# Hybrid attention encoder layer: keys, query reloads, denominators and w_out's rows moved in fewer, larger transfers

## The chip, the cores and the metric

The kernel runs on one core of one Trainium2 chip. The metric is the device time of one execution in microseconds. Three runs of the kernel before took 2543.44, 2537.59 and 2541.20 us, median 2541.2.

## What is computed

One encoder layer over x of 2048 tokens by 1024 columns, all in float32. An RMS norm and one projection give two head groups with 8 query heads and 2 key/value heads each, 64 columns a head. Group A attends over all tokens, group B over a window of 128 tokens to either side with a learned sink per head. Both go through one output projection, and a SwiGLU feed-forward part of 2816 columns follows. Cut to what matters here:

```python
h = rms_norm(x, norm_mix_pre[l])
qa, ka, va, qb, kb, vb = jnp.split(h @ w_in[l], SPLITS, axis=-1)
out_a = global_attention(rope(rms_norm(qa)), rope(rms_norm(ka)), va)
out_b = window_attention(rope(qb), rope(kb), vb, sink_b[l])     # den = sum(e) + exp(sink - m)
mixed = jnp.concatenate([rms_norm(out_a, group_norm_a[l]),
                         rms_norm(out_b, group_norm_b[l])], axis=-1) @ w_out[l]
x = x + rms_norm(mixed, norm_mix_post[l])
f = (jax.nn.silu(h2 @ w_gate[l]) * (h2 @ w_up[l])) @ w_down[l]  # h2: the norm of the new x
x = x + rms_norm(f, norm_ffn_post[l])
```

## The kernel before

The tokens are cut into 16 tiles of 128. Every float32 product is made of three or so passes over a high and a low half of its operands (names that end in h and l, or hi and lo).

**Projections, to about 412 us.** `proj` runs tile t through w_in into three PSUM banks (pp); `evac` copies them to nat on ScalarE. `rope` rotates queries and keys on VectorE and GpSimd, `heads(t)` transposes them. From there the keys of group A go to the DRAM scratch KD, the queries of group A to QA (high halves and low halves of both groups side by side), and the queries of group B are moved within SBUF into RB, four transfers of 64 rows a tile. Two tiles behind, group B is attended: `bmax` makes each head's maximum, negates it (mr) and moves it with the sink's exponentials (eh) into rows of R2B below the copied queries; `battn` makes scores, exponentials and output (o); `den_row` copies each group's row of denominators to rb and moves it to cmp, 8 rows of 64 a group, `recip` inverts cmp and writes it to RDB, `spread` reads it back over 64 partitions a group into rb, and `bfin` multiplies (oT) and stores OB. In tiles 4 to 11 `w_out_prep(k)` also loads part k of w_out in two halves of columns (woraw), scales and splits it (wohi on ScalarE, wolo on VectorE) and stores it to WO.

**Sweep of group A, to about 1200 us.** `attn` goes over 16 query tiles x 2 groups x 16 key tiles. `load_q(t)` reads R1 (group A's queries, high and low halves stacked) and R2 (the halves the other way round) from QA, called when tile t-1 is half done. The denominators go the same way as in group B, by the names cmpa, RDA and dena; the multiplication is oa<-oa,dena. The output projection runs beside it.

**Feed-forward, to the end**, with its own loads; the change does not touch it.

All transfers are issued by SyncE's queue. The order of all instructions on every engine comes from a planner (`Plan`, L257): it lays the recorded operations out by a table of costs, in which a transfer costs its bytes over 350 bytes a ns and 1100 ns, and SyncE 590 ns an issue, whatever its shape; the instructions then run on each engine in that order. Since one helper records them all, nearly all rows have the line L527, and one goes by the names.

`load` is one DMA. `ROWS` are the lower and upper 64 partitions. What sets a transfer's shape is the slice or rearrangement given to it, as here in `spread` and `w_out_prep` before:

```python
for g in range(2):
    src = scratch[8 * g:8 * g + 8].rearrange("(o c) x -> o (c x)", o=1)
    self.load(rb[ROWS[g]], src.broadcast_to([HD, 512]))
...
for h in range(2):
    self.load(raw[ROWS[h]], self.i["w_out"][r0 + 256 * h:r0 + 256 * h + HD, n * 512:(n + 1) * 512])
```

Of the kernel before, what the change touches and what calls it, by code (L numbers as in the profile page):

```python
# [18 lines left out]
P = 128  # L19
# [4 lines left out]
HD = 64  # L24
# [26 lines left out]
EARLY = 4  # L51
EARLY_NS = 2000
KV_NS = 3500
ES_ROW = 96
B0 = 432
B_TAIL = 13
T0_BANKS = (("mm", "ow", "o1"), ("mm", "a1", "a2"))
# [28 lines left out]
def f32(ap):  # L86
    return ap.bitcast(F32)
# [442 lines left out]
class Layer:  # L530
# [281 lines left out]
    def b_consts(self):  # L812
        nc, bp = self.nc, self.bp
        self.G = self.wp.tile([P, 2, 2, HD], F32, tag="G", bufs=1, name="G")
        for j, nm in enumerate(("q_norm_a", "k_norm_a")):
            self.bcast_row(self.G[:, j, 0, :], self.i[nm])
            self.bcast_row(self.G[:, j, 1, 0:32], self.i[nm][32:64])
            self.bcast_row(self.G[:, j, 1, 32:64], self.i[nm][0:32])
        nc.vector.tensor_scalar(self.G[:, 0], self.G[:, 0], 0.125, self.down_s, op0=ALU.mult, op1=ALU.mult)
        self.band = bp.tile([P, 3 * P], F32, tag="band", bufs=1, name="band")  # L820
        nc.gpsimd.memset(self.band, 0.0)
        for cs, sg in ((slice(0, P), 1), (slice(2 * P, 3 * P), -1)):
            nc.gpsimd.affine_select(out=self.band[:, cs], in_=self.band[:, cs], pattern=[[sg, P]],
                                    compare_op=ALU.is_ge, fill=-3.0e38, base=0, channel_multiplier=-sg)
        self.NR = 5
        self.VB = [bp.tile([P, 2, 2, P], F32R, tag=f"VB{r}", bufs=1, name=f"VB{r}") for r in range(self.NR)]
        self.K2B = [bp.tile([HD + 1, 2, P], F32R, tag=f"K2B{r}", bufs=1, name=f"K2B{r}") for r in range(self.NR)]
        for r in range(self.NR):
            nc.gpsimd.memset(f32(self.VB[r])[:, :, 0, HD:], 1.0)
            nc.gpsimd.memset(f32(self.VB[r])[:, :, 1, HD:], 0.0)  # L830
            nc.gpsimd.memset(f32(self.K2B[r])[HD:HD + 1], 1.0)
        self.va = [self.wp.tile([P, 2, 192], F32R, tag=f"va{r}", bufs=1, name=f"va{r}") for r in range(1)]
        for r in range(1):
            nc.gpsimd.memset(f32(self.va[r])[:, :, P:], 1.0)
        self.K1B, self.RB = {}, {}
        self.R2 = bp.tile([ES_ROW + 2, 2, 512], F32R, tag="R2B", bufs=1, name="R2B")
        nc.gpsimd.memset(f32(self.R2)[HD:ES_ROW + 2], 0.0)
        self.zs = bp.tile([ES_ROW + 2, P], F32R, tag="zs", bufs=1, name="zs")
        nc.gpsimd.memset(f32(self.zs), 0.0)
        nc.gpsimd.memset(f32(self.zs)[ES_ROW:ES_ROW + 2, HD:P], 1.0)  # L840

# [24 lines left out]
    def w_in_tiles(self, j):  # L868

        if j < 4:  # L870
            return [self.wk.tile([P, 512], F32R, tag=f"ks{3 * j + n}", bufs=1, name="w_in") for n in range(3)]
        w = (self.wk if j < 8 else self.wq).tile([P, 1536], F32R, tag=f"kv{j}", bufs=1, name="w_in")
        return [w[:, n * 512:(n + 1) * 512] for n in range(3)]

    def urgent(self, ns):
        if self.plan:
# [131 lines left out]
    def heads(self, t):  # L1008

        nc, wp, bp = self.nc, self.wp, self.bp  # L1010
        ra, rb = self.roped
        RB = bp.tile([P, 2, 512], F32R, tag="RB", bufs=3, name="RB")
        tk = self.mm_bank()[:, 0:2 * P].rearrange("p (a c) -> p a c", a=2)
        for j, src in ((1, rb), (0, ra)):
            nc.tensor.transpose(out=tk[:, j, :], in_=src[:, 8:10, :].rearrange("p h d -> p (h d)"),
                                identity=self.ident)
        KA = wp.tile([P, 2, P], F32R, tag="K1A", bufs=1, name="KA")
        nc.scalar.activation(KA[:, 0, :], tk[:, 0, :], AF.Copy)
        nc.vector.tensor_tensor(KA[:, 1, :], tk[:, 0, :], f32(KA)[:, 0, :], op=ALU.subtract)
        kd = self.k_part(self.KD[t // 2], t % 2).rearrange("p (g c) -> p g c", g=2)  # L1020
        k2b = self.K2B[t % self.NR]
        dst = []
        for s in ((t - 4) // 4, t // 4, (t + 4) // 4):
            pos = t - (4 * s - 1)
            if 0 <= s < NT // 4 and 0 <= pos < 6:
                if s not in self.K1B:
                    self.K1B[s] = bp.tile([P, 2, 6 * P], F32R, tag="K1B", bufs=2, name="K1B")
                dst.append(self.K1B[s][:, :, pos * P:(pos + 1) * P])
        for g in range(2):
            for h in range(2):  # L1030
                for d in dst:
                    nc.scalar.activation(d[ROWS[h], g, :], tk[ROWS[g], 1, :], AF.Copy)
            for h in range(2):
                self.load(kd[ROWS[g if h == 0 else 1 - g], g, :], f32(KA)[ROWS[g], h, :])
            nc.vector.tensor_tensor(k2b[0:HD, g, :], tk[ROWS[g], 1, :], f32(dst[0])[ROWS[g], g, :], op=ALU.subtract)
        yield 218
        for src, R in ((rb, RB), (ra, None)):
            tp = self.mm_bank()
            for p in range(4):
                nc.tensor.transpose(out=tp[:, p * P:(p + 1) * P],  # L1040
                                    in_=src[:, 2 * p:2 * p + 2, :].rearrange("p h d -> p (h d)"), identity=self.ident)
            HL = wp.tile([P, 2, 512], F32R, tag="RA", bufs=1, name="HL")
            nc.scalar.activation(HL[:, 0, :], tp, AF.Copy)
            nc.vector.tensor_tensor(HL[:, 1, :], tp, f32(HL)[:, 0, :], op=ALU.subtract)
            if R is None:
                self.load(self.QA[t], f32(HL))
            else:
                for g in range(2):
                    for h in range(2):
                        self.load(f32(R)[ROWS[g if h == 0 else 1 - g], g, :], f32(HL)[ROWS[g], h, :])  # L1050
            yield 436
        self.RB[t] = RB

# [7 lines left out]
    def bmax(self, t):  # L1061
# [1 line left out]
        nc, bp, sm = self.nc, self.bp, self.sm  # L1063
        RB = self.RB[t]
        R2 = self.R2
        for g in range(2):
            self.load(f32(R2)[0:HD, g, :], f32(RB)[ROWS[g], g, :])
        lo = 1 if t == 0 else 0
        hi = 2 if t == NT - 1 else 3
        n = (hi - lo) * P  # L1070
# [119 lines left out]
    def shifts(self):  # L1190

        nc, sm = self.nc, self.sm
        for t in range(NT):
            RA = [self.kv.tile([P, 512], F32R, tag="pha", bufs=NPH, name="RAs") for g in range(2)]
            for g in range(2):
                for h in range(2):
                    self.load(f32(RA[g])[ROWS[g if h == 0 else 1 - g]], self.QA[t][ROWS[g], h, :])
            mx = sm.tile([P, 8, 4], F32, tag="mx4", name="mx4")
            for h in range(8):
                g, p = h // 4, h % 4  # L1200
# [18 lines left out]
    def load_q(self, t):  # L1219
        if t >= NT or t in self.qt:  # L1220
            return
        R1 = self.kv.tile([P, 2, 512], F32R, tag="R1", name="R1")
        for g in range(2):
            for h in range(2):
                self.load(f32(R1)[ROWS[g if h == 0 else 1 - g], g, :], self.QA[t][ROWS[g], h, :])
        self.qt[t] = R1
        for g in range(2):
            R2 = self.wk.tile([P, 512], F32R, tag=f"ks{8 + (2 * t + g) % 4}", bufs=1, name="R2")
            for h in range(2):
                self.load(f32(R2)[ROWS[1 - g if h == 0 else g]], self.QA[t][ROWS[g], h, :])  # L1230
            self.qs[t, g] = R2

    def load_shift(self, t):
        self.sh_row[t] = self.kv.tile([1, 2, 512], F32R, tag="shr", bufs=1, name="shr")
# [30 lines left out]

    def den_row(self, rb, src, cmp, g):

        row = rb[HD * g:HD * g + 1]
        self.nc.scalar.activation(row, src[HD:HD + 1], AF.Copy)
        self.load(cmp[8 * g:8 * g + 8], row.rearrange("o (c x) -> o c x", x=HD))  # L1270

    def recip(self, cmp, scratch):
        self.nc.vector.reciprocal(cmp, cmp)
        self.load(scratch, cmp)

    def spread(self, rb, scratch):
        for g in range(2):
            src = scratch[8 * g:8 * g + 8].rearrange("(o c) x -> o (c x)", o=1)
            self.load(rb[ROWS[g]], src.broadcast_to([HD, 512]))

    def normalize(self, o, den, j):
        cs = slice(j * P, (j + 1) * P)
# [114 lines left out]
    def w_out_prep(self, k):  # L1397

        nc, bp = self.nc, self.bp
        r0 = 512 * (k // 4) + HD * (k % 4)  # L1400
        for n in range(2):
            raw = bp.tile([P, 512], F32, tag="pf", bufs=2, name="woraw")
            for h in range(2):
                self.load(raw[ROWS[h]], self.i["w_out"][r0 + 256 * h:r0 + 256 * h + HD, n * 512:(n + 1) * 512])
            hi = bp.tile([P, 512], F32R, tag="ph", bufs=PB, name="wohi")
            lo = bp.tile([P, 512], F32R, tag="pl", bufs=PB, name="wolo")
            nc.scalar.activation(hi, raw, AF.Copy, scale=self.gg[:, k:k + 1])
            nc.vector.scalar_tensor_tensor(lo, raw, self.gg[:, k:k + 1], f32(hi), op0=ALU.mult, op1=ALU.subtract)
            self.load(self.WO[2 * n][:, k], f32(hi))
            self.load(self.WO[2 * n + 1][:, k], f32(lo))  # L1410
            yield 500
# [425 lines left out]
```

## Time and profile before

| | |
|---|---|
| median of 3 runs | 2541.2 us (2537.59 to 2543.44) |
| the profiled execution | 2536.24 us, of which the span from first to last instruction 2534.4 us |
| TensorE matmuls busy | 2451.9 us (97%) |
| VectorE, GpSimd, ScalarE busy | 1894.7 us (75%), 1471.7 us (58%), 1392.5 us (55%) |
| mean share of the 16 DMA engines | 42.9% by the main queue, 349.40 MB in 200704 packets |
| mean granted TensorE clock | 0.993 of full |

The profile is of one execution. PE is TensorE, PEld its weight loads, ACT ScalarE, DVE VectorE, POOL GpSimd, SP SyncE. An engine's idle time costs something only where the engine that bounds the time waits for it in the end; which engine that is, is read for each stretch by itself.

### The profile page before, as it was taken

How to read it: one execution, taken by the hardware profiler on the slowest of the kernel's cores; microseconds unless marked ns; L12 is line 12 of the kernel's file. 1: busy time of each engine (PE TensorE's matmuls, PEld its weight loads, DVE VectorE, ACT ScalarE, POOL GpSimd, SP SyncE). 2: the span in 40 equal slices, each digit the busy share in tenths (PEclk: the TensorE clock that was granted, in tenths of full speed). 3: DMA queues.
4: the chain of work that ended last, by engine and by line, in shares of the span. 5: the costliest groups of instructions: out<-in, count | busy, mean ns of one | idle time of the engine just before them, and what ended most of it. 6: DMA issues, size and time to landing. Idle time of an engine off the chain costs nothing. (4 is left out here: it accounts for less than half of the span.)

```text
span 2534.4 us, 34148 instructions
## 1 busy us (share of the span) xinstructions
PE 2451.9 (97%) x10604; PEld 1946.2 (77%) x10604; DVE 1894.7 (75%) x2864; ACT 1392.5 (55%) x2610; POOL 1471.7 (58%) x1175
## 2 busy tenths in 40 slices
PE   8999999899999999999899999999999999999997
PEld 6777777567777777777688888878888888888886
DVE  6777776888898989898876776796656656556655
ACT  5666665797888888787433333353233334433433
POOL 4444333488889998999365566746546444331433
PEclk9999999999999999999999999999999999999999
DMA  6555545252221313231544444563333228554664
GB/s 208 152 174 166 168 144 168 80 195 65 76 80 58 106 59 104 96 121 63 195 135 145 162 154 162 190 222 104 101 107 104 92 79 278 175 182 143 194 189 153
DMA packets 200895, 351.66 MB, mean 139 GB/s; under 512 B 26624, under 2 KB 82304, under 8 KB 200192
## 3 DMA queue, kind: packets, MB, share of 16 engines
q1 hardware_dynamic: 200704, 349.40, 42.9%
q8 instruction: 85, 1.39, 0.2%
q14 instruction: 106, 0.87, 0.1%
HBM read 229.85 MB, written 106.56 MB: 133 GB/s over the span
## 5 line engine op out<-in xcount | busy, mean ns | idle before, releaser
L527 POOL TENSOR_TENSOR acc<-acc,pha 128x512 f32<-128x512 f32 x408 | 561.0, 1389 | 36.5 <-ACT pha L527 15.6
L527 POOL TENSOR_TENSOR s<-wraw 128x512 f32<-128x512 f32 x88 | 122.5, 1407 | 304.2 <-DMA wraw<-in_w_up_dram 184.3
L527 PE MATMUL gu<-xh,wl 128*128 128x512 f32 x776 | 288.4, 397 | 4.5 <-DVE wl L527 4.5
L527 PE MATMUL gu<-xl,wh 128*128 128x512 f32 x776 | 291.5, 396 | 0.0
L527 PE MATMUL gu<-xh,wh 128*128 128x512 f32 x776 | 287.4, 396 | 0.0
L527 DVE TENSOR_TENSOR pla<-mm,pha 128x512 fp32r<-128x512 f32 x370 | 246.4, 682 | 39.6 <-ACT pha L527 30.1
L527 PE MATMUL mm<-R,kt 128*128 128x512 f32 x740 | 256.0, 403 | 8.8 <-DVE pla L527 7.7
L527 ACT ACTIVATE wh<-s 128x512 fp32r<-128x512 f32 x176 | 110.6, 630 | 278.4 <-PE gu L527 141.4
L527 PE MATMUL pp<-w_in,xh 128*128 128x512 f32 x720 | 237.1, 403 | 12.6 <-ACT w_in L527 9.4
L527 DVE TENSOR_TENSOR al<-ar,ah 128x512 fp32r<-128x512 f32 x154 | 134.3, 874 | 149.3 <-ACT ah L527 128.5
L527 POOL TENSOR_TENSOR c<-c,c 128x512 f32<-128x512 f32 x132 | 201.7, 1542 | 69.5 <-DVE c L527 40.2
L527 ACT ACTIVATE mm<-mm 128x512 f32<-128x512 f32 x370 | 214.9, 590 | 29.1 <-PE mm L527 25.6
L527 ACT ACTIVATE ah<-ar 128x512 fp32r<-128x512 f32 x154 | 97.1, 630 | 220.2 <-PE gu L527 144.8
L527 DVE TENSOR_TENSOR c<-gu,c 128x512 f32<-128x512 f32 x174 | 116.4, 686 | 115.5 <-PE gu L527 114.1
L527 DVE TENSOR_TENSOR wl<-s,wh 128x512 fp32r<-128x512 f32 x176 | 175.6, 1003 | 12.1 <-ACT wh L527 5.9
L527 ACT ACTIVATE wh<-wraw 128x512 fp32r<-128x512 f32 x132 | 83.1, 630 | 175.3 <-PE gu L527 95.2
L527 PEld LDWEIGHTS gu<-xh,wl 128*128 128x128 f32 x776 | 146.6, 189 | 39.6 <-DVE wl L527 5.4
L527 PEld LDWEIGHTS mm<-R,kt 128*128 128x128 f32 x740 | 134.7, 189 | 53.3 <-DVE pla L527 25.8
L527 PE MATMUL gv<-xl,wh 128*128 128x512 f32 x456 | 173.2, 394 | 0.3 <-DVE xl L527 0.3
L527 PEld LDWEIGHTS gu<-xl,wh 128*128 128x128 f32 x776 | 146.4, 189 | 34.5
L527 PE MATMUL ow<-wo,oh 128*128 128x512 f32 x488 | 171.0, 396 | 1.8 <-DVE mix L527 0.9
L527 PEld LDWEIGHTS gu<-xh,wh 128*128 128x128 f32 x776 | 146.3, 189 | 34.4 <-ACT wh L527 0.2
(257 smaller groups left out, 6494.1 us busy)
## 6 DMA issues: line engine op xcount, KB each, us to landing
AC<-c SPq DMA_DIRECT2D x154, 256.0 KB
ar<-AC SPq DMA_DIRECT2D x154, 256.0 KB
wdr<-in_w_down_dram SPq DMA_DIRECT2D x99, 256.0 KB
wraw<-in_w_gate_dram SPq DMA_DIRECT2D x20, 1024.0 KB
wraw<-in_w_up_dram SPq DMA_DIRECT2D x20, 1024.0 KB
R<-QA SPq DMA_DIRECT2D x128, 128.0 KB
st<-XB SPq DMA_DIRECT2D x40, 256.0 KB
xn<-in_x_dram SPq DMA_DIRECT2D x16, 512.0 KB
```

What stands on the lines that cost most here:

```text
L527: op.call(*[real(a) for a in op.args], **{k: real(v) for k, v in op.kw.items()})
```

## The change

Eight kinds of transfer are cut in another way. With the shapes of the issues before and after, a tile each (out shape; the count of 2 is that of the slowest dimension on either side):

- KD<-KA: 4 of 64x128 become 2 of 2x64x128 (both groups in one, the halves no longer swapped for group 1).
- RB<-HL: still 4 of 64x512, now to the same half for both groups. R2B<-RB: 2 of 64x512 become 1 of 64x1024.
- R<-QA: 8 of 64x512 become 4 of 64x2x512; the second queries of both groups share one buffer (kq0, kq1), which takes the place of two (ks8 to ks11).
- cmp<-rb and cmpa<-dena: 2 of 8x64 become 1, read as 2x8x64. rb<-RDB and dena<-RDA: 2 of 64x512 become 1 to 128 rows, read as 2x64x512 (the 64 without a step).
- woraw<-w_out: 4 of 64x512 become 2 to 128 rows, read as 2x64x512.
- R2B's rows for the sink move up from 96 to 65, so that the last matmul of the denominators contracts 67 rows instead of 98.

```diff
-ES_ROW = 96
+ES_ROW = HD + 1
...
+    def w_in_slot(self, i):
+        if i < 8:
+            return self.wk.tile([P, 512], F32R, tag=f"ks{i}", bufs=1, name="w_in")
+        if i % 2 == 0:
+            self.pair = self.wk.tile([P, 2, 512], F32R, tag=f"kq{(i - 8) // 2}", bufs=1, name="w_in")
+        return self.pair[:, i % 2, :]
...
+        for h in range(2):
+            self.load(kd[ROWS[h]].rearrange("r g c -> g r c"), f32(KA)[:, h, :])
         for g in range(2):
...
-            for h in range(2):
-                self.load(kd[ROWS[g if h == 0 else 1 - g], g, :], f32(KA)[ROWS[g], h, :])
...
-                        self.load(f32(R)[ROWS[g if h == 0 else 1 - g], g, :], f32(HL)[ROWS[g], h, :])
+                        self.load(f32(R)[ROWS[h], g, :], f32(HL)[ROWS[g], h, :])
...
-        for g in range(2):
-            self.load(f32(R2)[0:HD, g, :], f32(RB)[ROWS[g], g, :])
+        self.load(f32(R2)[0:HD], f32(RB)[0:HD])
...
-        for g in range(2):
+        R2 = self.wk.tile([P, 2, 512], F32R, tag=f"kq{t % 2}", bufs=1, name="R2")
+        parts = self.QA[t].rearrange("(g r) h c -> h r g c", g=2)
+        for R, a in ((R1, 0), (R2, 1)):
             for h in range(2):
-                self.load(f32(R1)[ROWS[g if h == 0 else 1 - g], g, :], self.QA[t][ROWS[g], h, :])
+                self.load(f32(R)[ROWS[h ^ a]], parts[h])
...
-        row = rb[HD * g:HD * g + 1]
-        self.nc.scalar.activation(row, src[HD:HD + 1], AF.Copy)
-        self.load(cmp[8 * g:8 * g + 8], row.rearrange("o (c x) -> o c x", x=HD))
+        self.nc.scalar.activation(rb[HD * g:HD * g + 1], src[HD:HD + 1], AF.Copy)
+        if g == 1:
+            rows = rb.rearrange("(g r) (c x) -> g r c x", g=2, x=HD)[:, 0]
+            self.load(cmp, rows)
...
-        for g in range(2):
-            src = scratch[8 * g:8 * g + 8].rearrange("(o c) x -> o (c x)", o=1)
-            self.load(rb[ROWS[g]], src.broadcast_to([HD, 512]))
+        src = scratch.rearrange("(g c) x -> g (c x)", g=2)
+        self.load(rb, src.unsqueeze(1).broadcast_to([2, HD, 512]))
...
-            for h in range(2):
-                self.load(raw[ROWS[h]], self.i["w_out"][r0 + 256 * h:r0 + 256 * h + HD, n * 512:(n + 1) * 512])
+            rows = self.i["w_out"].rearrange("(a r) c -> a r c", r=256)[2 * (k // 4):2 * (k // 4) + 2]
+            self.load(raw, rows[:, HD * (k % 4):HD * (k % 4) + HD, n * 512:(n + 1) * 512])
```

The planner lays the whole program out anew. Two places are shown, both in tile 8, where part 4 of w_out is prepared.

SyncE before, from the move of group B's queries to the transfer of the negated maxima (x4 is four issues in a row):

```order
L527 DMA RB<-HL 64x512 x4
L527 DMA woraw<-in_w_out_dram 64x512 x4
L527 DMA R2B<-RB 64x512
L527 DMA QA_64<-HL 128x1024
L527 DMA KD_76<-KA 64x128
L527 DMA WO_89<-wohi 128x512
L527 DMA cmp<-rb 8x1x64
L527 DMA WO_91<-wohi 128x512
L527 DMA WO_90<-wolo 128x512
L527 DMA WO_92<-wolo 128x512
L527 DMA R2B<-mr 1x8x128
```

SyncE with the change, the same place:

```order
L527 DMA RB<-HL 64x512 x4
L527 DMA woraw<-in_w_out_dram 128x1x512
L527 DMA KD_76<-KA 2x64x128
L527 DMA woraw<-in_w_out_dram 128x1x512
L527 DMA WO_89<-wohi 128x512
L527 DMA R2B<-RB 64x1024
L527 DMA QA_64<-HL 128x1024
L527 DMA KD_76<-KA 2x64x128
L527 DMA cmp<-rb 16x1x64
L527 DMA WO_91<-wohi 128x512
L527 DMA WO_90<-wolo 128x512
L527 DMA WO_92<-wolo 128x512
```

R2B<-mr follows here too. A KD transfer now stands between the two loads of w_out (in 5 of the 8 parts), and the first store of WO, which waits for the first conversion, stands ahead of R2B<-RB.

ScalarE before, from the two conversions of w_out on:

```order
L527 ACTIVATE wohi<-woraw,gg 128x512 x2
L527 ACTIVATE nat<-pp,rstd 128x512
L527 ACTIVATE nat<-pp,rstd 128x2x128
L527 ACTIVATE mr<-mm 8x128
L527 ACTIVATE sq<-nat 128x640
```

ScalarE with the change:

```order
L527 ACTIVATE wohi<-woraw,gg 128x512
L527 ACTIVATE rb<-o_2682 1x512
L527 ACTIVATE oT<-o_2682 64x512
L527 ACTIVATE wohi<-woraw,gg 128x512
L527 ACTIVATE nat<-pp,rstd 128x512
L527 ACTIVATE mr<-mm 8x128
L527 ACTIVATE nat<-pp,rstd 128x2x128
```

The copies of the second group's denominators and output now stand between the conversions; nat and mr come behind the second one, as before.

## Rows read from the trace of the kernel before

**Rows 1.** The page, part 1: busy time and share of the span.
```profile
PE 2451.9 (97%) x10604; PEld 1946.2 (77%) x10604; DVE 1894.7 (75%) x2864; ACT 1392.5 (55%) x2610; POOL 1471.7 (58%) x1175
```

**Rows 2.** Stretch, its us; PE, PEld, DVE, ACT, POOL busy; clock, DMA share, GB/s.
```profile
113.60:325.30 211.70, 202.06 (x899) 157.16 (x899) 163.90 (x350) 136.28 (x290) 82.52 (x91) 1.00 0.56 175
210.20:239.20 29.00, 26.41 (x119) 20.26 (x118) 21.40 (x45) 19.11 (x42) 13.39 (x12) 1.00 0.55 169
411.60:463.00 51.40, 42.67 (x166) 30.47 (x165) 36.06 (x69) 25.46 (x53) 18.38 (x18) 0.90 0.69 201
540.00:1196.00 656.00, 636.72 (x2725) 496.49 (x2724) 580.99 (x859) 540.28 (x1005) 593.97 (x462) 0.99 0.28 95
```

**Rows 3.** Waits within 113.6 to 325.3: us in total, times, longest.
```profile
ACT wohi L527 <- DMA woraw<-in_w_out_dram: 10.0, 8, 2.6
...
DVE oT L527 <- DMA rb<-RDB: 1.4, 2, 0.8
```

**Rows 4.** By tile, SyncE's issues: ns min/median/max of one, first and last start.
```profile
L527 SPq DMA_DIRECT2D KD<-KA x64: 445/498/1120, 52.5 to 467.6; - x64
...
L527 SPq DMA_DIRECT2D R2B<-RB x32: 462/498/552, 55.7 to 499.4; - x32
...
L527 SPq DMA_DIRECT2D R<-QA x128: 444/587/1766, 415.1 to 1102.9; - x128
...
L527 SPq DMA_DIRECT2D woraw<-in_w_out_dram x32: 466/587/1228, 113.6 to 319.2; - x32
...
L527 SPq DMA_DIRECT2D cmp<-rb x32: 619/695/711, 87.9 to 523.4; - x32
...
L527 SPq DMA_DIRECT2D RDB<-cmp x16: 318/360/522, 93.0 to 526.5; - x16
...
L527 SPq DMA_DIRECT2D rb<-RDB x32: 465/532/595, 95.9 to 528.4; - x32
...
L527 SPq DMA_DIRECT2D dena<-RDA x30: 449/550/1205, 557.3 to 1189.2; - x30
```

**Rows 5.** DMA queues within 113.6 to 325.3: packets, MB, share of 16 engines.
```profile
q1 hardware_dynamic: 21194, 36.85, 56.0%
```

**Rows 6.** SyncE in order of time in tile 8: start us, us.
```profile
229.09 2.45 SPq L527 DMA_DIRECT2D woraw<-in_w_out_dram  x4
...
242.63 1.16 SPq L527 DMA_DIRECT2D rb<-RDB  x2
```

**Rows 7.** ScalarE, and TensorE's first score of group B, in tile 8.
```profile
232.78 0.72 ACT L527 ACTIVATE wohi<-woraw,gg 128x512 fp32r<-128x512 f32 x1
234.04 0.73 ACT L527 ACTIVATE wohi<-woraw,gg 128x512 fp32r<-128x512 f32 x1 [0.54 <-DMA woraw<-in_w_out_dram]
235.21 1.05 ACT L527 ACTIVATE nat<-pp,rstd 128x512 f32<-128x512 f32 x2 [0.45 <-PE pp L527]
236.15 0.25 ACT L527 ACTIVATE mr<-mm 8x128 fp32r<-8x128 f32 x1
...
240.14 0.47 PE L527 MATMUL mm<-R2B,K2B 65*128 65x512 f32 x1
```

**Rows 8.** VectorE in order of time in tile 8.
```profile
240.30 0.54 DVE L527 RECIPROCAL cmp<-cmp 16x64 f32<-16x64 f32 x1 [0.66 <-DMA cmp<-rb]
...
246.92 0.68 DVE L527 TENSOR_TENSOR oT<-oT,rb 128x512 f32<-128x512 f32 x1
```

**Rows 9.** SyncE and VectorE in order of time in the sweep, one tile.
```profile
941.75 1.72 SPq L527 DMA_DIRECT2D dena<-RDA  x2
...
942.24 0.69 DVE L527 CAST pha<-mm 128x512 fp32r<-128x512 f32 x1
...
945.92 1.24 DVE L527 TENSOR_TENSOR oa<-oa,dena 128x512 f32<-128x512 f32 x1 [0.47 <-DMA dena<-RDA]
```

**Rows 10.** By tile R2B: matmuls of 65 and of 98 rows.
```profile
L527 PE MATMUL mm<-R2B,K2B x92: 391/398/504, 77.1 to 509.0; 65*128 65x512 f32 x92
...
L527 PE MATMUL o<-R2B,zs x32: 389/399/628, 86.8 to 521.9; 98*128 98x512 f32 x32
```

More of the change, by code (lines that the diff above doesn't have):

```diff
@@ L836, in b_consts @@
         self.R2 = bp.tile([ES_ROW + 2, 2, 512], F32R, tag="R2B", bufs=1, name="R2B")
-        nc.gpsimd.memset(f32(self.R2)[HD:ES_ROW + 2], 0.0)
         self.zs = bp.tile([ES_ROW + 2, P], F32R, tag="zs", bufs=1, name="zs")
         nc.gpsimd.memset(f32(self.zs), 0.0)
-        nc.gpsimd.memset(f32(self.zs)[ES_ROW:ES_ROW + 2, HD:P], 1.0)
+        nc.gpsimd.memset(f32(self.zs)[HD:ES_ROW + 2, HD:P], 1.0)
+        nc.gpsimd.memset(f32(self.zs)[HD:HD + 1, HD:P], 0.0)
     def load_w_in(self, k0, k1):
@@ L870, in w_in_tiles @@
         if j < 4:
-            return [self.wk.tile([P, 512], F32R, tag=f"ks{3 * j + n}", bufs=1, name="w_in") for n in range(3)]
+            return [self.w_in_slot(3 * j + n) for n in range(3)]
         w = (self.wk if j < 8 else self.wq).tile([P, 1536], F32R, tag=f"kv{j}", bufs=1, name="w_in")
         return [w[:, n * 512:(n + 1) * 512] for n in range(3)]
+    def w_in_slot(self, i):
[4 more added lines that the diff above has]
+        return self.pair[:, i % 2, :]
     def urgent(self, ns):
@@ L1196, in shifts @@
                 for h in range(2):
-                    self.load(f32(RA[g])[ROWS[g if h == 0 else 1 - g]], self.QA[t][ROWS[g], h, :])
+                    self.load(f32(RA[g])[ROWS[h]], self.QA[t][ROWS[g], h, :])
             mx = sm.tile([P, 8, 4], F32, tag="mx4", name="mx4")
@@ L1222, in load_q @@
         R1 = self.kv.tile([P, 2, 512], F32R, tag="R1", name="R1")
-        for g in range(2):
+        R2 = self.wk.tile([P, 2, 512], F32R, tag=f"kq{t % 2}", bufs=1, name="R2")
+        parts = self.QA[t].rearrange("(g r) h c -> h r g c", g=2)
+        for R, a in ((R1, 0), (R2, 1)):
             for h in range(2):
-                self.load(f32(R1)[ROWS[g if h == 0 else 1 - g], g, :], self.QA[t][ROWS[g], h, :])
+                self.load(f32(R)[ROWS[h ^ a]], parts[h])
         self.qt[t] = R1
         for g in range(2):
-            R2 = self.wk.tile([P, 512], F32R, tag=f"ks{8 + (2 * t + g) % 4}", bufs=1, name="R2")
-            for h in range(2):
-                self.load(f32(R2)[ROWS[1 - g if h == 0 else g]], self.QA[t][ROWS[g], h, :])
-            self.qs[t, g] = R2
+            self.qs[t, g] = R2[:, g, :]
     def load_shift(self, t):
@@ L1399, in w_out_prep @@
         nc, bp = self.nc, self.bp
-        r0 = 512 * (k // 4) + HD * (k % 4)
         for n in range(2):
             raw = bp.tile([P, 512], F32, tag="pf", bufs=2, name="woraw")
-            for h in range(2):
-                self.load(raw[ROWS[h]], self.i["w_out"][r0 + 256 * h:r0 + 256 * h + HD, n * 512:(n + 1) * 512])
+            rows = self.i["w_out"].rearrange("(a r) c -> a r c", r=256)[2 * (k // 4):2 * (k // 4) + 2]
+            self.load(raw, rows[:, HD * (k % 4):HD * (k % 4) + HD, n * 512:(n + 1) * 512])
             hi = bp.tile([P, 512], F32R, tag="ph", bufs=PB, name="wohi")
```

## The prediction

> **What bounds the kernel now.** I read the busy times first, then the stretches of the program, then the waits, then the transfers. The busy times say that TensorE is the bound: it works 97% of the span [rows 1]. So a transfer costs only where something that TensorE needs comes late. The stretches tell where that can be [rows 2]. While w_out is prepared beside the projections (113.6 to 325.3 us) TensorE is idle for 211.7 - 202.1 = 9.6 us; between the projections and the attention sweep (411.6 to 463.0) for 8.7 us; in the sweep itself (540 to 1196) for 19.3 us. ScalarE and VectorE are busy 64% and 77% of the first of these stretches, so they have holes there, but both run in a fixed order: an instruction that waits for a transfer holds up all behind it. The waits show that this happens already [rows 3]: in this stretch ScalarE stands still 10.0 us, in 8 of its 16 conversions of w_out (wohi), for woraw. VectorE waits for the spread denominators (rb) 1.4 us only. There is hardly slack behind woraw, and little behind rb.
>
> **What the change removes.** By the counts of transfers, KD goes from 64 to 32, R2B<-RB from 32 to 16, R<-QA from 128 to 64, woraw and cmp and rb from 32 to 16 each, cmpa and dena from 30 to 15 each: 190 issues less, of 0.5 to 0.7 us each on SyncE [rows 4], some 110 us of its time over the run. SyncE is no bound in the stretches above, so this is worth only what those issues delay. The one place where they stand in front of idle TensorE is the first tile's query load between 411.6 and 463.0: 4 of 8 issues go, 4 x 0.59 = 2.4 us. I take **2 us gained**, between 0 and the 8.7 us of idle there.
>
> **What it adds.** Four kinds of transfer (KD, woraw, cmp/cmpa, rb/dena) now have on one side an outermost count of 2 (two groups or two halves), where they had 64, 64, 8 and 64. The other transfers that were merged keep 64 outermost. No transfer in this trace begins with 2, so the price has two ends: such a transfer is dealt over all 16 engines like its neighbours, or over two.
>
> The rate of one engine comes from the stretch of w_out: 36.85 MB took 56.0% of 16 engines for 211.7 us [rows 5, 2], 36.85 MB / (0.560 x 16 x 211.7 us) = 19.4 KB per us and engine. 256 KB (woraw, rb, dena) then take 0.84 us over 16 engines and 128 KB / 19.4 = **6.75 us** over two; KD's 64 KB take 0.21 us or 1.7 us.
>
> Which end? The nearest rows are transfers that begin with 8, and the trace treats them apart: cmp<-rb moves 2 KB in 8 pieces and is issued in 0.695 us (median), while RDB<-cmp moves 4 KB in 16 pieces and is issued in 0.360 us [rows 4]. Every kind with 64 outermost stays near 0.5 to 0.6. So the outermost count, not the bytes, decides how a transfer is dealt out, and 2 lies further down from 16 than 8 does. I take the two-engine end.
>
> The Trainium skill, "DMA: Bandwidth & Descriptors", section "Why a DMA increments its semaphore by 16 and not by 1", states it as a rule: a transfer runs on the largest number of engines, at most 16, that divides the outermost counts above 1 of both sides; for 128 and 2 that is two. By it the sum is the one made here; no row here shows a count of 2.
>
> **The sum.** (a) woraw, 8 parts of w_out. Before, the four issues start at 229.09 and the second conversion runs at 234.04 [rows 6, 7]. Over two engines the two loads follow each other there: 2 x 6.75 = 13.5 us instead of 1.7, less two issues saved (1.2 us): the second conversion comes 10.6 us later. On ScalarE the evacuation of the projection's banks (nat) and the negated maxima (mr) stand behind it, 235.21 and 236.15, and TensorE's first score of group B's attention, which reads mr, at 240.14 [rows 7]; the order after the change keeps wohi, wohi, nat, mr. Both ends: 0 if ScalarE's 36% of idle took it up, 10.6 if nothing does. Since half of the conversions wait already, I take 9. 8 x 9 = **72 us** (0 to 85).
>
> (b) rb, 16 tiles of group B. It lands 6.75 - 0.84 - 0.6 (one issue) = 5.3 us later. Before, VectorE's reciprocal runs at 240.30 and the multiplication that reads rb at 246.92 [rows 8]; the last rb load is issued at about 243.2 [rows 6]. In this tile's new order the multiplication comes nine rows after the reciprocal instead of thirteen, so it is asked for no later than before, finds rb some 5 us late, and the rope's products and the subtractions of the next probabilities stand behind it. VectorE is busy 77%, so part is caught up. Ends 0 and 16 x 5.3 = 85; I take 3 a tile, **48 us**.
>
> (c) dena, 15 tiles of the sweep. It lands 5.3 us later too. At 941.75 the load is issued and at 945.92 the multiplication had waited for it [rows 9]; after the change 8 to 30 rows of VectorE lie between reciprocal and multiplication, at some 0.7 us each (a cast there took 0.69 [rows 9]): enough in the 8 tiles with 11 rows or more, 3 us or so short in the other 7, and VectorE is busy 89% of the sweep [rows 2]. Ends 0 and 80; I take **10 us**.
>
> (d) KD: 1.5 us more each, 32 of them. Nobody waits for KD until the keys are read back, but in 5 of the 8 parts one stands between the two woraw: 5 x 1.7 = **8 us** (0 to 47).
>
> (e) The clock. Where TensorE was idle for 17% (411.6 to 463.0) the granted clock was 0.90 of full [rows 2]. A tile with 12 us of waiting in some 41 is idle more than that; at 0.1 x 41 us a tile that is up to 33 us over eight. TensorE waits anyway in part of it: **10 us**.
>
> At nothing: the reload of the sweep's second queries now takes one buffer for both groups; it is asked for half a tile ahead, which covers it (cover gone: four issues, some 2.4 us a tile). The shorter contraction of the denominators' last matmul: 98 and 65 rows take the same 0.40 us [rows 10]. cmp and cmpa are 2 KB.
>
> 72 + 48 + 10 + 8 + 10 - 2 = 146 us. The profiled execution took 2536.2 us, so **2682 us**; the median of the runs shown, 2541.2, lies 5 us above that execution.
>
> A check by the engines' load alone: a tile of w_out's stretch is 29.0 us and fills an engine for 0.55 x 29.0 = 16.0 us [rows 2]. Two engines lose 2.9 us of that (their sixteenth of woraw, rb and KD) and gain 2 x 6.75 + 6.75 + 2 x 1.7 = 23.7: 36.8 us of work in 29.0. So they are over-full by 7.8 us a tile; (a) and (b) together, 12 us, lie above this floor.
>
> **The rivals.**
> 1. Dealt over 16 engines. Then only fewer issues and fewer completions remain, and the change ends on the other side: the 10.0 us of ScalarE and the 1.4 of VectorE [rows 3] shrink, TensorE gets back part of its 9.6 us idle and 2 us at the sweep's start: about 6 us, 2530 us. For it: the bytes are the same and the destination is 128 partitions. Against: the issue times of transfers that begin with 8 [rows 4]. It decides from 8 engines upward, where 256 KB take 1.7 us, less than the landings waited for today. Beside it stands the Trainium skill, same page, section "Rules for kernel authors": two transfers to disjoint halves of the partitions are better made one of 128. By that rule the time would be this rival's.
> 2. Two engines, but everything is hidden except their load: 8 x 7.8 = 63 us, 2599 us. For it: 36% and 23% idle on ScalarE and VectorE. Against: half of the conversions wait today [rows 3].
> 3. Nothing is covered: 85 + 85 + 80 + 47 + 33 = 330 us, 2866 us. For it: TensorE's own idle is only 9.6 us in the stretch. Against: VectorE's slack in the sweep, and waits of several engines that overlap.
>
> **How the numbers follow.** Chances: the forecast 0.58, rival 1 0.12, rival 2 0.18, rival 3 0.12. The range 2590 to 2790 holds the forecast, rival 2 and the lower part of rival 3; rival 1 and the rest of rival 3, together under 0.2, stay outside. A measurement of this kernel can tell about 0.2% (5 us) from no change; rival 1 straddles that bound: faster 0.07, same 0.05, slower 0.88. That two of the merged kinds, R<-QA and R2B<-RB, get cheaper for certain does not turn the sign: their whole worth is in the 2 us.
>
> **What would show it.** In the profile after: the stretch of w_out's eight parts 65 to 130 us longer, with TensorE idle there 80 us or more instead of 9.6; ScalarE's wait for woraw at 70 to 90 us instead of 10.0; VectorE's wait for rb at 50 us or more over the run; woraw's and rb's issues at about 0.7 us instead of 0.59 and 0.53. Bytes stay as they are. The sweep from 540 on should keep its length within 20 us, and all after 1300 its own. The prediction is wrong if woraw's wait stays near 10 us (rival 1), if it grows but TensorE's idle does not (rival 2), or if the sweep grows by 50 us or more (rival 3).

## The result, and the profile after

The changed kernel takes 2697.94 us (median of 4 runs, 2690.86 to 2699.31) against 2539.70 (4 runs, 2537.59 to 2543.44): ratio 1.0615, 95% interval 1.060 to 1.063. By that ratio it is 156 us slower; the forecast was 2682 us in a range of 2590 to 2790. The profiled execution took 2690.86 us, its span 2689.0.

The page's part 1, the busy times of the changed kernel:

```profile
PE 2503.6 (93%) x10604; PEld 1978.5 (74%) x10604; DVE 1887.8 (70%) x2864; ACT 1392.3 (52%) x2610; POOL 1471.8 (55%) x1175
```

Every engine runs as many instructions as before; against [rows 1] only TensorE's busy time grew (its matmuls by 52 us, its weight loads by 32; the granted clock is 0.970 of full on average instead of 0.993), and its share fell from 97% to 93%. The rest of the added time is waiting. Where it lies shows in the stretches: the stretch of w_out, one of its tiles, and 656 us of the sweep that start as long after the last rb load as those of [rows 2] (columns as there).

```profile
114.00:423.10 309.10, 236.47 (x908) 178.44 (x907) 156.99 (x354) 139.59 (x295) 88.88 (x92) 0.86 0.38 121
256.20:298.50 42.30, 33.04 (x126) 24.97 (x125) 21.86 (x48) 19.27 (x43) 13.68 (x14) 0.82 0.37 119
...
674.70:1330.70 656.00, 629.31 (x2683) 487.98 (x2682) 572.61 (x848) 532.11 (x990) 579.38 (x453) 0.99 0.30 94
```

The stretch of w_out went from 211.7 to 309.1 us. TensorE is idle for 309.1 - 236.5 = 72.6 us of it instead of 9.6, and a tile lasts 42.3 us instead of 29.0. The sweep is nearly what it was: 26.7 us idle of 656 instead of 19.3. The DMA engines as a whole became less busy in w_out's stretch, 38% instead of 56%. So the transfers are not late for want of engines in general. The waits in this stretch, in us, times, longest:

```profile
ACT wohi L527 <- DMA woraw<-in_w_out_dram: 80.4, 16, 6.1
DVE wolo L527 <- ACT wohi L527: 69.5, 16, 6.1
...
DVE oT L527 <- DMA rb<-RDB: 33.8, 7, 7.8
PE pp L527 <- ACT nat L527: 29.3, 8, 4.8
```

All 16 conversions of w_out wait for their load, 5.0 us each; before, 8 of them did, 1.25 us each [rows 3]. The last row is how much of this reaches TensorE: the projection waits for nat, which stands behind the second conversion. It is the largest of TensorE's waits there, 29.3 of 72.6 us idle; behind it come waits for VectorE, 19.0 us for mx and 13.1 for pl. Over the whole run VectorE waits 71.8 us for rb:

```profile
DVE oT L527 <- DMA rb<-RDB: 71.8, 16, 7.8
```

The same tile 8 that [rows 6 to 8] show before, now SyncE first, then ScalarE, VectorE and TensorE (start us, us, in brackets what its engine waited for):

```profile
278.31 0.61 SPq L527 DMA_DIRECT2D woraw<-in_w_out_dram  x1
278.97 0.55 SPq L527 DMA_DIRECT2D KD<-KA  x1
281.00 1.67 SPq L527 DMA_DIRECT2D woraw<-in_w_out_dram  x1
...
300.43 0.55 SPq L527 DMA_DIRECT2D rb<-RDB  x1
```

```profile
286.28 0.72 ACT L527 ACTIVATE wohi<-woraw,gg 128x512 fp32r<-128x512 f32 x1 [4.60 <-DMA woraw<-in_w_out_dram]
...
293.24 0.72 ACT L527 ACTIVATE wohi<-woraw,gg 128x512 fp32r<-128x512 f32 x1 [5.01 <-DMA woraw<-in_w_out_dram]
293.87 0.67 ACT L527 ACTIVATE nat<-pp,rstd 128x512 f32<-128x512 f32 x1
294.43 0.25 ACT L527 ACTIVATE mr<-mm 8x128 fp32r<-8x128 f32 x1
```

```profile
308.19 0.69 DVE L527 TENSOR_TENSOR oT<-oT,rb 128x512 f32<-128x512 f32 x1 [3.37 <-DMA rb<-RDB]
308.80 0.69 DVE L527 TENSOR_TENSOR pl<-pf,ph 128x512 fp32r<-128x512 f32 x1
```

```profile
294.59 1.22 PE L527 MATMUL pp<-w_in,xh 128*128 128x512 f32 x2 [4.79 <-ACT nat L527]
...
309.54 0.80 PE L527 MATMUL o<-pl,VB 128*128 128x512 f32 x1 [3.01 <-DVE pl L527]
...
310.99 0.63 PE L527 MATMUL mm<-R2B,K2B 65*128 65x512 f32 x1
```

From the first issue of w_out to the second conversion 14.9 us pass (278.31 to 293.24); before it was 4.95 (229.09 to 234.04, [rows 6, 7]). nat follows at once, and TensorE, which had waited 4.79 us, goes on at 294.59. Later rb is issued at 300.43 and its reader runs at 308.19; pl stands behind it, and TensorE waits 3.01 us for pl. TensorE's other waits between 276 and 311 us are 1.5 us and less.

Two stretches of the same tile tell more (columns as in [rows 2]): the time in which the count-2 loads of w_out are under way and little else, and the time right behind TensorE's 3.01 us of idle.

```profile
282.00:286.00 4.00, 4.00 (x19) 3.35 (x18) 2.54 (x10) 0.00 (x0) 0.00 (x0) 1.00 0.14 50
```

```profile
309.50:312.00 2.50, 2.46 (x6) 1.98 (x7) 1.52 (x5) 2.13 (x4) 0.63 (x2) 0.50 0.28 105
```

In the first, the DMA engines are busy 0.14 on average, at 50 GB/s; two busy engines of 16 would be 0.125, and 50 GB/s over two are 25 KB per us and engine. In the second, TensorE's granted clock is 0.50 of full, the lower of its two levels (1.2 and 2.4 GHz).

The issue times of the merged transfers, in the view by tile (ns min/median/max, first and last start):

```profile
L527 SPq DMA_DIRECT2D woraw<-in_w_out_dram x16: 544/609/3539, 114.0 to 406.0; - x16
...
L527 SPq DMA_DIRECT2D cmp<-rb x16: 535/558/3222, 89.5 to 657.9; - x16
...
L527 SPq DMA_DIRECT2D rb<-RDB x16: 520/550/558, 93.9 to 663.1; - x16
```

They are issued about as fast as the ones with 64 outermost (587 and 532 ns, [rows 4]), and cmp faster than the one with 8 (558 against 695 ns).

### The profile page after: what moved, and what is told of

Read it like the earlier page. It is cut to its first block, busy times and chain, and to the rows that moved or that the text cites. A ratio compares the mean times of both kernels' runs of the same rounds, so it can differ in the third digit from the quotient of the medians.

```text
span 2689.0 us, 33809 instructions
## 1 busy us (share of the span) xinstructions
PE 2503.6 (93%) x10604; PEld 1978.5 (74%) x10604; DVE 1887.8 (70%) x2864; ACT 1392.3 (52%) x2610; POOL 1471.8 (55%) x1175
## 4 chain that ended last, share of the span: by engine, by line
PE 55%; DVE 3%; issue 1%; DMA 1%; ACT 1%; POOL 0%; SPq 0%; DVEq 0%; POOLq 0%; ACTq 0%
PE gu L527 29%; PE gv L527 17%; PE ow L527 3%; PE mm L527 2%; PE o L527 2%; PE a L527 2%; DVE pla L527 1%; DVE wl L527 1%; DVE st L527 0%; DVE xl L527 0%; DMA dena<-RDA 0%; DMA AC<-c 0%; DVE c L527 0%; DMA wraw<-in_w_gate_dram 0%; DMA wdr<-in_w_down_dram 0%
## 5 line engine op out<-in xcount | busy, mean ns | idle before, releaser
L527 PE MATMUL pp<-w_in,xh 128*128 128x512 f32 x720 | 256.5, 433 | 40.3 <-ACT nat L527 30.6
L527 PE MATMUL gu<-xh,wl 128*128 128x512 f32 x776 | 279.3, 396 | 5.7 <-DVE wl L527 5.7
L527 PE MATMUL gu<-xl,wh 128*128 128x512 f32 x776 | 280.9, 396 | 0.0
L527 PEld LDWEIGHTS pp<-w_in,xh 128*128 128x128 f32 x720 | 147.6, 209 | 80.6 <-ACT nat L527 36.0
L527 PE MATMUL gv<-xh,wl 128*128 128x512 f32 x456 | 168.4, 395 | 5.1 <-DVE wl L527 5.1
```

The costliest lines, as they stand in the source:

```text
L527: op.call(*[real(a) for a in op.args], **{k: real(v) for k, v in op.kw.items()})
```

## The experiments

Two theories stood against each other. **Few engines:** a transfer whose outermost count is 2 is dealt over two engines, and it is this lateness alone, of four kinds of transfer (KD, woraw, rb, dena; cmp and cmpa also begin with 2 now, but move only 4 KB), that costs. **Something else in the change:** the planner's new order, the merged buffers, or the two loads in one transfer. Most of the kernels below are the kernel before with its own order, in which only a transfer's outermost count is altered by another walk over the same bytes. A worth is the ratio less 1, times the median of the kernel before in the same set of runs (2543.15 in the first, 2540.83 in the second, 2540.91 in the third). Code is shown in short form.

### The loads of w_out, outermost 2, 4 and 16

```diff
-  self.load(raw[ROWS[h]], self.i["w_out"][r0 + 256 * h:...])
+  rows = self.i["w_out"][r0 + 256 * h:...]
+  self.load(raw[ROWS[h]], rows.rearrange("(r a) c -> a r c", a=2))   # 4 and 16 in the others
```

Outermost 2: 

> The kernel before, with its own order and its own four loads of w_out a part; only the source of each load is walked as 2 x 32 rows instead of 64 (rows 0, 2, 4, .. then 1, 3, 5, ..), so that its outermost count is 2. Same bytes, same pieces of 2 KB, same number of issues; the rows of w_out are permuted within a head's 64, so the output is another one. Theory 1 (a count of 2 deals a transfer over two engines): four loads of 128 KB follow each other on two engines, 4 x 3.4 = 13.5 us a part instead of 1.7, ScalarE's wait for woraw goes from 10.0 to 80 us or more, the time to 2540 + 70..105 = 2610 to 2645. Theory 2 (the merging or the planner's new order cost the time, not the count): within 6 us of before.

Outermost 16, the control: 

> Control to the run with 2 x 32 rows: the same edit with 16 x 4 rows (rows 0, 16, 32, 48, then 1, 17, ..; w_out's rows permuted within a head), outermost count 16. Theory 1: sixteen engines, within 6 us of before, ScalarE's wait for woraw near 10 us. If instead the interleaved walk over DRAM rows is what costs, it is slow like the run with 2 x 32.

Outermost 4: 

> As the run with w_out's loads walked as 2 x 32 rows, but 4 x 16 (rows of w_out permuted within a head). Theory 1, the engines are as many as the count: four loads of 128 KB over four engines are 4 x 1.7 = 6.75 us a part, against 13.5 with two and 1.7 with sixteen; ScalarE's wait for woraw 25 to 55 us; 2543 + 10..40. Rival A (any count under 16 falls to the same slow path): as slow as 2 x 32, 2605 or more. Rival B (only a count under 4 hurts): within 5 us of before.

Measured: 2611.50 us with 2 (ratio 1.0269, 1.0254 to 1.0285, 68 us), 2570.28 with 4 (1.0118, 1.0102 to 1.0135, 30 us), 2543.22 with 16 (1.0002, 0.9992 to 1.0012, nothing). The waits for woraw with 2, with 4 and with 16, each from its own trace:

```profile
ACT wohi L527 <- DMA woraw<-in_w_out_dram: 76.0, 16, 7.5
```

```profile
ACT wohi L527 <- DMA woraw<-in_w_out_dram: 38.8, 15, 4.7
```

```profile
ACT wohi L527 <- DMA woraw<-in_w_out_dram: 6.9, 7, 1.8
```

Same kernel, same issues, same bytes, and by the traces the same instructions in the same order on every engine: the outermost count alone makes the wait.

The DMA queue over the whole run with 2, with 4 and with 16 (packets, MB, share of 16 engines), each from its own page; before it was 200704 packets and 349.40 MB:

```profile
q1 hardware_dynamic: 200256, 349.40, 41.7%
```

```profile
q1 hardware_dynamic: 200320, 349.40, 42.1%
```

```profile
q1 hardware_dynamic: 200704, 349.40, 42.9%
```

There are 32 such loads in a run, so each has 448 / 32 = 14 packets fewer with 2, 384 / 32 = 12 fewer with 4 and none fewer with 16, with the same bytes. That is what comes out if every engine that takes part adds one small packet to a load: 16 engines before, 2, 4 and 16 here. The runs with rb, dena and KD at 2 below fit too: 14 packets fewer for each of their 32, 30 and 64 transfers (200256, 200284 and 199808 packets).

Tile 8 with 2, SyncE and ScalarE:

```profile
262.78 2.54 SPq L527 DMA_DIRECT2D woraw<-in_w_out_dram  x4
```

```profile
270.99 0.72 ACT L527 ACTIVATE wohi<-woraw,gg 128x512 fp32r<-128x512 f32 x1 [4.55 <-DMA woraw<-in_w_out_dram]
276.21 0.72 ACT L527 ACTIVATE wohi<-woraw,gg 128x512 fp32r<-128x512 f32 x1 [4.49 <-DMA woraw<-in_w_out_dram]
```

and with 4:

```profile
244.79 2.45 SPq L527 DMA_DIRECT2D woraw<-in_w_out_dram  x4
```

```profile
250.38 0.72 ACT L527 ACTIVATE wohi<-woraw,gg 128x512 fp32r<-128x512 f32 x1 [1.94 <-DMA woraw<-in_w_out_dram]
254.04 0.72 ACT L527 ACTIVATE wohi<-woraw,gg 128x512 fp32r<-128x512 f32 x1 [2.94 <-DMA woraw<-in_w_out_dram]
```

From first issue to second conversion: 4.95 us before, 9.25 with 4, 13.43 with 2. Over all eight tiles the delays add up to 26 us with 4 and 63 us with 2, and 30 and 68 were measured: the second conversion's lateness is paid in full, and 4 or 5 us more. With 2 the two conversions, 256 KB apart, are 5.2 us apart: 256 KB / (2 x 5.2 us) = 24.6 KB per us and engine if two carry them.

### The denominators and the keys

```diff
-  self.load(rb[ROWS[g]], src.broadcast_to([HD, 512]))
+  self.load(rb[ROWS[g]], src.unsqueeze(0).broadcast_to([2, HD // 2, 512]))   # rb in one, dena in the other
...
-  self.load(kd[ROWS[...], g, :], f32(KA)[ROWS[g], h, :])
+  self.load(kd[ROWS[...], g, :].rearrange("(r a) c -> a r c", a=2), f32(KA)[ROWS[g], h, :])   # KD, a third
```

rb: 

> The kernel before in its own order and with its own two loads a tile; only group B's denominators (rb) are read with a source walked as 2 x 32 instead of 64 (the same row over and over, so the values stay). Theory 1 (two engines): each tile's rb lands 5 to 6 us later, VectorE's wait for rb goes from 3.8 to 60 us or more; the forecast put 3 us a tile on the path, 48 in all; 2543 + 30..70. Rival (VectorE's idle hides it): within 10 us of before while VectorE's wait grows all the same.

dena: 

> The kernel before; only the sweep's denominators (dena) are read with a source walked as 2 x 32. The forecast's term (c): 10 us, as VectorE's 11% of idle in the sweep takes up most. The run with all four kinds at a count of 2 had a sweep 40 us longer than before, so theory 1 now expects 2543 + 20..45. Rival (the longer sweep of that run came from what the projections left behind, not from dena): within 8 us of before.

KD: 

> The kernel before; only KD's 64 transfers are written as 2 x 32 rows (the keys' 64 components are permuted within a half, so the output is another one). Nobody waits for KD inside the projections. Theory 1: each takes two engines 0.8 us instead of 0.1, 2543 + 0..12. Rival (what lies behind KD on those engines is late): 20 us or more.

Measured: rb 2616.29 us (1.0299, 1.0282 to 1.0316: 76 us), dena 2563.89 (1.0103, 1.0082 to 1.0123: 26 us), KD 2545.80 (1.0008, 0.9991 to 1.0024: not told from nothing). The waits of the first two, each from its own trace:

```profile
DVE oT L527 <- DMA rb<-RDB: 70.5, 14, 7.0
```

```profile
DVE oa L527 <- DMA dena<-RDA: 27.2, 9, 4.6
```

VectorE's wait is nearly the whole loss in both: 70.5 of 76 us (3.8 of waiting before) and 27.2 of 26. What VectorE loses at this place it doesn't win back. For KD the price depends on its neighbour. In the order of before, a KD transfer of 32 KB stands between w_out's loads in parts 1, 5 and 6. With w_out alone at 2 the two conversions are 5.2 to 5.4 us apart in all eight parts; with all four kinds at 2 (the next run), in the same order, they are 5.9 to 6.3 us apart in these three parts and 5.2 to 5.6 in the others. In the changed order a KD transfer of 64 KB stands between the two loads of w_out in parts 0, 3, 4, 5 and 7: there the conversions are 6.7 to 7.0 us apart (6.96 in tile 8 above, which has part 4), in the parts 1, 2 and 6, without it, 5.2 to 5.5 (by the starts of the 16 conversions). Part 2 as an example of these, ScalarE of the changed kernel:

```profile
204.53 0.72 ACT L527 ACTIVATE wohi<-woraw,gg 128x512 fp32r<-128x512 f32 x1 [4.46 <-DMA woraw<-in_w_out_dram]
209.99 0.72 ACT L527 ACTIVATE wohi<-woraw,gg 128x512 fp32r<-128x512 f32 x1 [4.74 <-DMA woraw<-in_w_out_dram]
```

So a KD of 64 KB makes the load behind it about 1.5 us later, some 7 us for the five parts; that is read from part to part and wasn't tried by itself in the changed order.

### All four with 2, nothing merged

> The kernel before in its own order, nothing merged; KD, woraw, rb and dena each walked with an outermost count of 2 on one side (KD and woraw by permuting rows within 64, so keys of group A and rows of w_out are permuted and the output is another one; rb and dena unchanged in value). Theory 1: the change's whole loss without the change's merging or order, 2540 + 120..175 = 2660 to 2715. Theory 2: within 10 us of before.

Measured: 2708.06 us (1.0643, 1.0623 to 1.0664: 164 us). The kernel before, in its own order and with all its issues, becomes as slow as the changed one, a little slower even, by the outermost counts alone. The four worths alone add up to 68 + 76 + 26 + 2 = 172 us, so they hardly overlap.

### The changed kernel with parts put back

```diff
-  rows = self.i["w_out"].rearrange("(a r) c -> a r c", r=256)[...]
-  self.load(raw, rows[:, ...])
+  for h in range(2):
+      self.load(raw[ROWS[h]], self.i["w_out"][r0 + 256 * h:...])
```

Only w_out's loads put back: 

> The changed kernel with only the loads of w_out put back (four of 64x512 a tile); KD, rb and dena keep their count of 2. Theory: the loads of w_out cost in the change what they cost alone (68 us), so 2698 - 68 = 2630 us (2610 to 2645), ScalarE's wait for woraw back at 10 to 15 us, and TensorE's idle in the stretch of w_out about halved. Rival: the two engines stay over-full by rb and KD, and the waits only move to rb; then the gain is under 35 us (over 2663).

Measured: 2635.37 us (1.0364, 1.0343 to 1.0386, 92 us), 64 us below the changed kernel, each against the kernel before (156 - 92). Its waits for the two:

```profile
DVE oT L527 <- DMA rb<-RDB: 60.9, 16, 7.6
...
ACT wohi L527 <- DMA woraw<-in_w_out_dram: 9.0, 8, 2.5
```

and its stretch of w_out:

```profile
115.30:364.50 249.20, 215.34 (x911) 166.93 (x909) 156.30 (x355) 142.28 (x296) 90.54 (x92) 0.95 0.49 150
```

The wait for woraw is back at 9.0 us, that for rb stays; TensorE's idle there is 33.9 us instead of 72.6, about half. So the first theory's numbers hold; the loss that is left is that of rb, dena and KD, and of what else changed, the order above all.

All four kinds put back (R<-QA, R2B<-RB, cmp and cmpa stay merged, R2B's rows stay at 65): 

> The changed kernel with those transfers put back that began with 2: woraw, rb, dena in two halves, KD in four; R<-QA, R2B<-RB, cmp and cmpa stay merged, R2B stays at 67 rows. Theory 1: the loss is gone and what is left is the worth of fewer issues, 2530 to 2540 us against 2540 before, a gain of 0 to 0.4%. Theory 2 (order): it stays above 2560, as most of the merging and the new order are still there.

Measured: 2559.12 us (1.0060, 1.0046 to 1.0074): 15 us slower than before, where a small gain was expected. Three of its waits:

```profile
DVE cmp L527 <- DMA cmp<-rb: 10.4, 9, 2.9
...
ACT wohi L527 <- DMA woraw<-in_w_out_dram: 5.6, 8, 1.7
...
DVE oT L527 <- DMA rb<-RDB: 4.0, 3, 2.3
```

Those for woraw and rb are about what they were before (10.0 and 3.8 us) or less, and in its sweep (560 to 1180 us) no wait for a transfer is listed at all. Of the merged transfers that are left, cmp is waited for longer, 10.4 us instead of 2.7, and it still begins with 2; whether the merge or the order makes this wait isn't shown here. What differs too is the planner's order, from the first instructions on. Against the kernel with only w_out put back, the three other kinds are worth 92 - 15 = 77 us in the changed kernel, as far as the orders of the two allow.

### The planner's order alone

```diff
-                avail["SP"] = start + 590
+                avail["SP"] = start + 570      # and 610
```

570, in the kernel before: 

> The kernel before with one number of its planner changed: SyncE's issue is counted as 570 ns instead of 590. No transfer and no shape changes; the order of the instructions does, on every engine. Theory: the new order alone is what made the run with all 64-outermost merges 16 us slower; then this kernel is off the one before too, by 5 to 20 us, in either direction. Rival: the merged transfers themselves cost those 16 us; then the order hardly matters and this kernel stays within 4 us (2537 to 2546).

610, in the kernel before: 

> The same with 610 ns instead of 590. Theory (the order alone): off by 5 to 20 us, and by another amount than with 570. Rival (the merged transfers): within 4 us of the kernel before.

610, in the changed kernel with all four kinds put back: 

> The changed kernel with its four kinds of count 2 put back (KD, woraw, rb, dena), as in the run that took 2559, and the planner's issue of SyncE counted as 610 ns instead of 590. Theory (the order alone): another time than 2559, by 5 us or more, and perhaps level with the kernel before. Rival (the merged transfers cost 16 us): 2555 to 2563 again.

Measured: 2553.22 us (1.0042, 1.0026 to 1.0057), 2563.90 (1.0084, 1.0069 to 1.0099) and 2565.03 (1.0088, 1.0073 to 1.0103). The kernel before loses 11 and 21 us by another order in which no transfer, shape or count is changed; the 15 us of the kernel with all four kinds put back lie between, and 610 makes them 22. The wait for cmp is 12.4 us with 570 in the kernel before, where cmp is not merged, so an order alone can make that wait as well. So the run with all four kinds put back doesn't speak against the merges that are left, and not for them: what they win or cost can't be told from what a new order does. None of the twelve kernels beats the kernel before.

### Where each loses its time

From the first and last issues in the views by tile. Each column is the time in us since the one to its left: from the start to the first load of w_out, from there to its last load, on to the last rb, to the last dena, to the end.

| kernel | first w_out | last w_out | last rb | last dena | end |
|---|---|---|---|---|---|
| before | 113.6 | 205.6 | 209.2 | 660.8 | 1345.2 |
| changed | 114.0 | 292.0 | 257.1 | 665.6 | 1360.3 |
| w_out with 2 | 114.6 | 261.8 | 220.2 | 662.4 | 1346.6 |
| rb with 2 | 118.2 | 240.5 | 248.0 | 664.6 | 1347.5 |
| dena with 2 | 113.1 | 205.3 | 209.6 | 681.9 | 1350.2 |
| all four with 2 | 119.7 | 293.6 | 257.5 | 685.6 | 1349.0 |
| changed, w_out put back | 115.3 | 239.6 | 236.7 | 672.9 | 1369.7 |
| changed, all four put back | 113.5 | 208.1 | 213.0 | 654.6 | 1367.6 |
| before, planner's 610 | 115.0 | 210.4 | 210.8 | 670.0 | 1356.4 |

w_out's loads cost where w_out is loaded, rb's over all of group B, dena's in the sweep. The changed kernel loses 86 us up to w_out's last load, 48 from there to the last rb, 5 to the last dena, and 15 behind it, where the feed-forward lies, which the change doesn't touch; the last two rows lose 22 and 11 us in that last stretch too, without any of the four kinds at a count of 2.

## Why the prediction was right, and where its steps were not

- **The sign and the size: right.** 2682 forecast, 2697.94 measured; the mechanism of the forecast, two engines for an outermost count of 2, is what the runs show: 68, 30 and 0 us for 2, 4 and 16. The profile names no engine for a packet, but three readings agree on two: twice the count, about half the delay; 14 packets fewer a load; and a busy share of 0.14 of 16 in tile 8 while such loads are under way.
- **How close the sum came is in part luck.** 146 us were forecast and 156 measured. By the kernels with parts put back the 156 are 64 for w_out's loads (72 forecast), 77 for rb, dena and KD together (48 + 10 + 8 = 66), and 15 that are left, where the forecast had 10 for the clock and 2 gained. What one term has too much others have too little, and 11 to 21 us of a new order were in no term at all.
- **"Which end?": the right end by the wrong evidence.** The prediction argued from issue times, and expected 0.7 us for the new shapes. They are issued in 0.55 to 0.61 us, like those with 64; cmp, which now begins with 2 on its source, even faster than with 8. The issue time says nothing about the count. The rows that were chosen didn't hold what was needed to decide; the runs with other counts did.
- **The rate of an engine: too low.** 19.4 KB per us, from an average over the stretch; two conversions 256 KB apart are 5.2 to 5.5 us apart where nothing stands between, 23 to 25 KB per us and engine, so about 5.3 us for 256 KB instead of 6.75.
- **(a) woraw: 72 forecast, 68 alone and 64 within the change.** 10.6 us of delay were forecast a tile; 10.0 are found in tile 8 and 8.7 on average over the eight, KD's share in it. ScalarE's idle share took up next to nothing, as taken: alone, 63 us of delay cost 68.
- **(b) rb: 48 forecast, 76 alone: the term that was mis-sized most.** The step that failed is "VectorE is busy 77%, so part is caught up". 76 / 16 = 4.8 us a tile come through, of the 5.3 that were forecast as the upper end. Tile 8 of the changed kernel shows why: VectorE's order puts pl right behind the multiplication, TensorE needs pl at once, so the 23% of idle lie at other places. With rb alone at 2, TensorE waits 39.6 us for pl; before it was 5.9. The 76 us were measured in the order of before, but VectorE's wait for rb in the changed kernel is as long (71.8 us against 70.5).
- **(c) dena: 10 forecast, 26 alone.** The forecast was made for the changed order, the 26 us were measured in the order of before, so they don't refute it. In the changed kernel VectorE waits 11.1 us for dena instead of 27.2, and the sweep is 5 us longer; dena by itself wasn't tried there.
- **(d) KD: 8 forecast, about 7 by the five parts that have one in between;** alone, in the old order, none that can be told.
- **(e) the clock: 10 forecast, not found as a term of its own.** The granted clock did fall, to 0.86 of full in w_out's stretch (1.00 before), and TensorE's matmuls there took 34 us more (236.5 against 202.1). Tile 8 shows when: after 3.01 us of idle the granted clock is 0.50 and the next matmuls take 0.63 us instead of 0.40. But with w_out's loads alone the transfers' lateness over the eight tiles, 63 us, is already nearly the whole loss of 68, with a clock that fell nearly as far (0.88 from 114.6 to 391.0). So most of the slower matmuls must lie in time in which a transfer was waited for, and about 5 us are left for them there. This is argued from the traces; a run with the clock alone wasn't tried.
- **At nothing: cmp.** The forecast gave it no price because it is small. In the changed kernel VectorE waits 14.9 us for it over the run, before 2.7; as said above, a new order alone can do nearly that much, so what this term is worth stays open.
- **The 2 us gained: not seen.** A new order outweighs it: it cost 11 and 21 us in the runs that change nothing else.
- **The rivals.** 1 (dealt over 16) fell: all sixteen conversions wait. Beside it stood the Trainium skill's rule, "DMA: Bandwidth & Descriptors", section "Rules for kernel authors", that two transfers to disjoint halves of the partitions are better made one. Here that cost 64 us for w_out; the measurement decides, and the rule on the outermost count in the same page, cited in the prediction, agrees with 2, 4 and 16 (68, 30 and 0 us) and goes before it. 2 (all hidden but the load, 63 us) fell by 93 us. 3 (nothing covered, 330 us) came true for rb alone: 76 of 85.
- **What would show it.** In range: w_out's stretch (97 us longer), ScalarE's wait (80.4), VectorE's wait (71.8), the bytes, the sweep's length (665.6 against 660.8 from the last rb to the last dena). Off: TensorE's idle in the stretch, 72.6 us for "80 or more"; the issue times; and "after 1300 unchanged", where 15 us came in. The change doesn't touch that part, and two runs without the four kinds lose 22 and 11 us there, so the new order is the likely cause; it isn't shown for this run.

## What to carry to other kernels

Before two transfers are merged, look at the outermost count that the merged one has on either side: two halves put in front make a 2 of a 64, and the larger transfer then comes some 5 us later, as here, while bytes and issue time look the same or better. Merge so that the large count stays outermost (16 was as good as 64 here), or leave two transfers. An engine's idle share is no cover for a wait in a fixed order: look for what stands right behind the waiting instruction, and who needs that at once; and where a planner lays the program out anew, run it with a neutral change of its numbers before a few us are put down to the edit.

## What was not expected of the hardware

- The issue on SyncE doesn't tell how a transfer is dealt out: 0.609 us (woraw, count 2), 0.587 (count 64), 0.562 (count 2 in the order of before). The number of packets on the page does: 14 fewer for each load with 2, 12 fewer with 4.
- A transfer of 64 KB that begins with 2 delays the one behind it by about 1.5 us though the 16 engines are busy 38% on average: an average share over all engines hides a queue on a few.
